# Chunked recurrences of a hybrid decoder step: the weights inside chunks computed in one run of 32-column matmuls per head

## Chip, cores and metric

One core of one Trainium2 chip. The metric is device microseconds (us) of one execution of the whole program, lower is better.

## What is computed

One inference step of a two-layer decoder for a prompt of 512 tokens and eight samples of 4 new tokens, 544 rows in all, width 2048. Layer A runs an attention (NSA) and a gated linear recurrence (GLA, 4 heads, key width 128, value width 256) side by side; layer C is HGRN2 (16 heads, key and value width 128). Both layers use this recurrence:

```python
def gated_recurrence(q, k, v, log_a, s0):
    """S_t = diag(exp(log_a_t)) S_{t-1} + k_t^T v_t, o_t = q_t S_t, per head"""
    ...
    def step(s, xs):
        qc, kc, vc, gc = xs
        b = jnp.cumsum(gc, axis=2)
        decay = jnp.exp(jnp.where(causal, b[:, :, :, None, :] - b[:, :, None, :, :], -jnp.inf))
        att = jnp.einsum('bhik,bhijk,bhjk->bhij', qc, decay, kc)
        o = jnp.einsum('bhij,bhjv->bhiv', att, vc) + jnp.einsum('bhik,bhkv->bhiv', qc * jnp.exp(b), s)
        b_last = b[:, :, -1:, :]
        s = jnp.exp(b_last)[:, :, 0, :, None] * s + jnp.einsum('bhjk,bhjv->bhkv', kc * jnp.exp(b_last - b), vc)
        return s, o
```

Around it stand the input projections `h @ w_in`, the output projections `o @ w_out`, root mean square norms and silu gates.

## The kernel before

**Layout.** Activations stand transposed, features in the 128 partitions and the 544 tokens along the free axis (`TP` = 512 prompt columns, `TS` = 32 sample columns). A big projection is a row of blocks of 128 output columns (`gemm_block`, L355). A block takes 16 K-tiles; a K-tile is six matmuls of 128x272 (weights split in a high and a low part, two halves of the tokens), so a block is 96 matmuls into a PSUM tile tagged `gm`. `stream` (L296) takes the weights in pieces of four K-tiles: it loads them in 512 KB transfers, splits each piece into `wh` (ScalarE) and `wl` (VectorE), and calls the split of piece n+2 ahead of the matmuls of piece n (`split_to(n + 3)`).

**Order of the work.** The program writes each engine's instructions in a fixed order, worked out while it is built. A planner clock `clk` follows TensorE: each matmul adds a cost (`mm`, L197), each VectorE or ScalarE operation has a modelled duration (`account`, L144). Every other job is a generator in a lane; `pump` is called behind each K-tile and steps the lanes whose wake time has come. A generator yields `self.at(tiles, banks=n)`: the modelled time at which these tiles are ready plus 200 ns, and n of the four small PSUM banks (tag `s`) are free. `together(gens, width)` (L688) interleaves up to `width` generators. TensorE therefore runs the long `gm` stream with short groups of small matmuls put in behind K-tiles.

**A head's recurrence** (`recurrence`, L713, called by `gla_task` and `hgrn_task` in lane H, one head after the other). The 512 prompt tokens are four chunks of 128. The lower triangle of weights inside a chunk is put together from levels, each a pair of factor tiles (differences of the cumulative log decay `b`, exponentials on ScalarE, products with `k` and `q` on VectorE), a group of small fp32 matmuls (each fp32 matmul is two records in the trace), and copies out of PSUM:

- `local` (L735): 4x4 blocks from factors `d` (a tile named `lv`) and `qh`; 16 matmuls of 32 stationary and 32 moving columns, and one for the samples into a second bank; masked copies into `attD` and `ats`.
- `level(4)` (L784): 16 matmuls of 32 by 16 columns; a masked copy into `attD`.
- `middle` (L828): 16 matmuls of 32 by 48 columns, moving tile `lq`; three masked copies into `attD`.
- `level(32)`: 8 matmuls of 32 by 32 columns; two copies into `attT`.
- `level(64)`: 4 matmuls of 64 by 64 columns; two copies into `attT`.

All of them use `tile_position=(0, 32 * g)`: the matmul occupies 32 (or 64) columns of the array from that position. Each level takes a bank of its own. `values` (L758) transposes the values and makes block-diagonal copies `vbd` for the samples; `passing` (L858) makes the factors that carry the state from chunk to chunk (`qe`, `ke`, `ket`, `kes`). The order is

```python
        gens = [local()] + [values(j) for j in range(nv)] + [level(4), middle(), level(32), level(64)] + [passing()]
        yield from self.together(gens, 3)
```

with four copies of `attD` onto the diagonal of `attT` behind it (L901), then the outputs (`prompt_out`, `sample_out`), the norm (`sq`, `sqh`, `sql`) and `y`. In layer C the first block of head h needs the flag of head h-2; the z block of head h-3 comes behind each head from the fourth on. Layer C ends with the z blocks of heads 13 to 15, and the output projection's last quarter needs the gated output of every head, split into `oh` and `ol`.

Of the kernel before, what the change touches and what calls it, by code (L numbers as in the profile page):

```python
# [20 lines left out]
P = 128  # L21
D = 2048
KT = D // P
TP = 512
NB = 8
NS = 4
TS = NB * NS
T = TP + TS
# [66 lines left out]
class Kern:  # L95
# [617 lines left out]
    def recurrence(self, q, k, la, vT, s0, out_p, out_s, gn, done):  # L713


        nc, ident = self.nc, self.ident
        nv = len(vT)
# [6 lines left out]
        attT, attD, ats = self.att  # L724
        yield self.at(la)
        b = self.r("b")
        nc.vector.tensor_tensor_scan(b, self.reset, la, 0.0, op0=ALU.mult, op1=ALU.add)

        d = self.r("lv")
# [3 lines left out]
        idb = [None]  # L733

        def local():  # L735
            yield self.at(d)
            qh = self.r("qh")
            nc.scalar.activation(qh, d, AF.Exp)
            nc.scalar.activation(d, d, AF.Exp, scale=-1.0)
            yield self.at(qh)  # L740
            self.tt(qh, qh, q, ALU.mult)
            yield self.at(d)
            self.tt(d, d, k, ALU.mult)
            yield self.at(d, qh, banks=2)
            ps, ps2 = self.bank(), self.bank()
            for c, g, rows, x in blocks32():
                self.mm(ps[rows, c * 32:(c + 1) * 32], d[:, x:x + 32], qh[:, x:x + 32], tile_position=(0, 32 * g))
            self.mm(ps2[:TS, :TS], d[:, TP:T], qh[:, TP:T])
            yield self.at(ps, attD)
            mk = self.lmask[1].unsqueeze(1).to_broadcast([P, 4, 32])  # L750
            nc.vector.copy_predicated(attD, mk, ps[:, :P].rearrange("p (c i) -> p c i", c=4))
            nc.vector.copy_predicated(ats, self.lmask[1][:TS], ps2[:TS, :TS])

        def blocks32():

            return [(c, g, slice(32 * g, 32 * g + 32), c * P + 32 * g) for c in range(4) for g in range(4)]

        def values(j):  # L758

            v3 = self.thrice(vT[j])  # L760
            yield self.at(vT[j], banks=1)
            ps = self.bank()
            for c in range(4):
                self.tr(ps[:, c * P:(c + 1) * P], vT[j][:, c * P:(c + 1) * P], ident)
            t = self.r("vt", [P, 4, P])
            self.cp(t, ps.rearrange("p (c d) -> p c d", c=4))
            vt.append(t)
            yield self.at(v3, banks=1)
            ps = self.bank(reads=3)
            self.tr(ps[:3 * TS, :P], v3, ident)  # L770
            t = self.sm("vs", [TS, P], bufs=2)
            nc.scalar.copy(t, ps[:TS, :P])
            vs.append(t)
            t = self.sm("v3", [3 * TS, P], bufs=2, dt=F32R)
            nc.scalar.copy(t, ps[:3 * TS, :P])
            yield self.at(t)
            nc.vector.tensor_tensor(t[2 * TS:], ps[2 * TS:3 * TS, :P], t[2 * TS:].bitcast(F32), op=ALU.subtract)
            for hf in range(2):
                vb = self.r("vbd", [P, 4, P], dt=F32R)
                self.tt(vb[:3 * TS], t.bitcast(F32).unsqueeze(1).to_broadcast([3 * TS, 4, P]),  # L780
                        self.bmask[:, hf * 4:hf * 4 + 4].unsqueeze(2).to_broadcast([3 * TS, 4, P]), ALU.mult)
                vbd.append(vb)

        def level(s):  # L784

            d = self.r("lv")
            v = lambda t: t[:, :TP].rearrange("p (n two s) -> p n two s", two=2, s=s)
            L, Rr = (lambda t: v(t)[:, :, 0, :]), (lambda t: v(t)[:, :, 1, :])
            n = 256 // s
            cb = v(b)[:, :, 0, s - 1:s].to_broadcast([P, n, s])  # L790
            nc.vector.tensor_tensor(Rr(d), Rr(b), cb, op=ALU.subtract)
            nc.vector.tensor_tensor(L(d), cb, L(b), op=ALU.subtract)
            yield self.at(d)
            nc.scalar.activation(d[:, :TP], d[:, :TP], AF.Exp)
            yield self.at(d)
            self.tt(L(d), L(d), L(k), ALU.mult)
            self.tt(Rr(d), Rr(d), Rr(q), ALU.mult)
            yield self.at(d, banks=1)
            ps = self.bank(reads=1 if s == 4 else 2)
            if s == 4:  # L800
                for c, g, rows, x in blocks32():
                    rr = d[:, x:x + 32].rearrange("p (n two s) -> p n two s", two=2, s=s)[:, :, 1, :]
                    self.mm(ps[rows, c * 16:(c + 1) * 16], d[:, x:x + 32], rr, tile_position=(0, 32 * g))
                yield self.at(ps, attD)
                nc.vector.copy_predicated(attD.rearrange("p c (n two s) -> p c n two s", two=2, s=s)[:, :, :, 1, :],
                                          self.lmask[4].unsqueeze(1).to_broadcast([P, 4, 4, 4]),
                                          ps[:, :64].rearrange("p (c n s) -> p c n s", c=4, s=s))
            elif s == 32:
                for c in range(4):
                    for g in (0, 2):  # L810
                        x = c * P + 32 * g
                        self.mm(ps[32 * g:32 * g + 32, c * 32:(c + 1) * 32], d[:, x:x + 32], d[:, x + 32:x + 64],
                                tile_position=(0, 32 * g))
                yield self.at(ps, attT)
                for r in (0, 64):
                    self.cp(attT[r:r + 32, :, r + 32:r + 64], ps[r:r + 32, :P].rearrange("p (c i) -> p c i", c=4))
            else:

                for c in range(4):
                    x, r = c * P, 64 * (c % 2)  # L820
                    self.mm(ps[r:r + 64, (c // 2) * 64:(c // 2) * 64 + 64], d[:, x:x + 64], d[:, x + 64:x + 128],
                            tile_position=(0, r))
                yield self.at(ps, attT)
                for r in range(2):
                    self.cp(attT[0:64].rearrange("p (a b) i -> p b a i", b=2)[:, r, :, 64:128],
                            ps[64 * r:64 * r + 64, :P].rearrange("p (c i) -> p c i", c=2))

        def middle():  # L828

            d, e = self.r("lv"), self.R.tile([P, 16, 48], F32, name=self.nm("lq"), tag="lq", bufs=1)  # L830
            b4 = b[:, :TP].rearrange("p (n m s) -> p n m s", m=4, s=8)
            bn = b[:, :TP].rearrange("p (n s) -> p n s", s=32)
            qn = q[:, :TP].rearrange("p (n s) -> p n s", s=32)
            nc.vector.tensor_tensor(d[:, :TP].rearrange("p (n m s) -> p n m s", m=4, s=8),
                                    b4[:, :, :, 7:8].to_broadcast([P, 16, 4, 8]), b4, op=ALU.subtract)
            quarters = [(0, 24), (24, 16), (40, 8)]
            for m, (x, w) in enumerate(quarters):
                nc.vector.tensor_tensor(e[:, :, x:x + w], bn[:, :, 32 - w:], bn[:, :, 8 * m + 7:8 * m + 8].to_broadcast([P, 16, w]),
                                        op=ALU.subtract)
            yield self.at(e)  # L840
            nc.scalar.activation(d[:, :TP], d[:, :TP], AF.Exp)
            nc.scalar.activation(e, e, AF.Exp)
            yield self.at(e)
            self.tt(d[:, :TP], d[:, :TP], k[:, :TP], ALU.mult)
            for x, w in quarters:
                self.tt(e[:, :, x:x + w], e[:, :, x:x + w], qn[:, :, 32 - w:], ALU.mult)
            yield self.at(d, e, banks=1)
            ps = self.bank(reads=3)
            for c, g, rows, x in blocks32():
                self.mm(ps[rows, c * 48:(c + 1) * 48], d[:, x:x + 32], e[:, 4 * c + g, :], tile_position=(0, 32 * g))  # L850
            yield self.at(ps, attD)
            for m, (x, w) in enumerate(quarters):
                nc.vector.copy_predicated(attD[:, :, 32 - w:], self.lmask[8][:, m:m + 1].unsqueeze(2).to_broadcast([P, 4, w]),
                                          ps[:, :192].rearrange("p (c i) -> p c i", c=4)[:, :, x:x + w])

        passed = {}

# [38 lines left out]
            yield self.at(kes)  # L896
            nc.vector.tensor_tensor(kes[TS:2 * TS], ps[TS:2 * TS, :P], kes[TS:2 * TS].bitcast(F32), op=ALU.subtract)

        gens = [local()] + [values(j) for j in range(nv)] + [level(4), middle(), level(32), level(64)] + [passing()]
        yield from self.together(gens, 3)  # L900
        yield self.at(attD, attT)  # L901
        for g in range(4):
            s = slice(32 * g, 32 * g + 32)
            self.cp(attT[s, :, s], attD[s])
        qe, dl, ket, kes = passed["qe"], passed["dl"], passed["ket"], passed["kes"]
        os_ = []

# [53 lines left out]
        gens = []  # L961
# [23 lines left out]
        for h in range(2):  # L985
            ps = self.bank()
# [1167 lines left out]
```

## Time and profile before

| | |
|---|---|
| runs | 2386.69, 2389.62, 2389.16 us; median 2389.16 |
| profiled execution | 2390.82 us, of it 2389.1 us span |
| TensorE granted clock, mean | 0.991 of full speed |
| TensorE matmul | 2341.7 us busy, 20560 records |
| VectorE / ScalarE | 1382.0 / 1022.8 us busy |
| DMA | mean 113 GB/s |

How to read it: a share over the span is a mean over stages. The timeline merges equal neighbours into one row (start, length, xcount); the length of such a row reaches to the end of its last record, and matmul ends are modelled and overlap the next start. Distances between starts are what can be added.

### The profile page before, as it was taken

How to read it: one execution, taken by the hardware profiler on the slowest of the kernel's cores; microseconds unless marked ns; L12 is line 12 of the kernel's file. 1: busy time of each engine (PE TensorE's matmuls, PEld its weight loads, DVE VectorE, ACT ScalarE, POOL GpSimd, SP SyncE). 2: the span in 40 equal slices, each digit the busy share in tenths (PEclk: the TensorE clock that was granted, in tenths of full speed). 3: DMA queues.
4: the chain of work that ended last, by engine and by line, in shares of the span. 5: the costliest groups of instructions: out<-in, count | busy, mean ns of one | idle time of the engine just before them, and what ended most of it. 6: DMA issues, size and time to landing. Idle time of an engine off the chain costs nothing.

```text
span 2389.1 us, 49910 instructions
## 1 busy us (share of the span) xinstructions
PE 2341.7 (98%) x20560; PEld 2247.9 (94%) x20560; DVE 1382.0 (58%) x2948; ACT 1022.8 (43%) x2152; POOL 25.7 (1%) x79
## 2 busy tenths in 40 slices
PE   7899999999999999999999999999999999999997
PEld 7799999999999988779999999999999999999997
DVE  5355567774664653354335667777777666665333
ACT  5244344443443443343333445544455444454333
POOL 3000000000000000000000000000000000000000
PEclk9899999999999999999999999999999999999999
DMA  7755434444213135454443233333333333333333
GB/s 247 241 161 158 124 99 109 106 111 119 54 50 89 43 108 163 147 164 134 134 124 98 85 98 101 92 98 90 91 98 94 95 91 91 98 90 113 99 113 111
DMA packets 433612, 270.68 MB, mean 113 GB/s; under 512 B 16285, under 2 KB 419640, under 8 KB 433256
## 3 DMA queue, kind: packets, MB, share of 16 engines
q1 hardware_dynamic: 432520, 257.05, 37.3%
q0 software_dynamic: 256, 8.32, 1.0%
q8 instruction: 162, 2.65, 0.5%
q10 hardware_dynamic: 608, 2.11, 0.2%
q14 instruction: 66, 0.54, 0.1%
HBM read 234.34 MB, written 41.42 MB: 115 GB/s over the span
## 4 chain that ended last, share of the span: by engine, by line
PE 93%; DVE 2%; DMA 1%; SPq 1%; ACT 1%; issue 1%; DVEq 0%; ACTq 0%
PE gm L211 77%; PE s L211 12%; PE s L215 4%; SPq L84 1%; DMA wr<-in_a_w_in_dram 1%; DVE ol L84 1%; DVE wl L84 1%; DMA xres<-res 0%; ACT sq L84 0%; ACT wh L84 0%; DMA wr<-in_a_w_out_dram 0%; ACT e L84 0%; DVE e L84 0%; ACT fr L84 0%; ACT qs L84 0%
## 5 line engine op out<-in xcount | busy, mean ns | idle before, releaser
L211 PE MATMUL gm<-xh,wh 128*128 128x272 f32 x3744 | 814.1, 299 | 1.9 <-ACT wh L84 1.9
L211 PE MATMUL gm<-xh,wl 128*128 128x272 f32 x3744 | 776.1, 289 | 2.7 <-DVE wl L84 2.7
L211 PE MATMUL gm<-xl,wh 128*128 128x272 f32 x3744 | 776.3, 289 | 0.0
L84 DVE TENSOR_TENSOR wl<-wr,wh 128x512 fp32r<-128x512 f32 x660 | 449.8, 686 | 492.4 <-ACT wh L84 491.1
L211 PEld LDWEIGHTS gm<-xh,wh 128*128 128x128 f32 x3744 | 587.1, 189 | 22.7 <-issue 11.6
L84 ACT CAST wh<-wr 128x512 fp32r<-128x512 f32 x660 | 402.4, 616 | 480.7 <-PE gm L211 459.8
L211 PEld LDWEIGHTS gm<-xh,wl 128*128 128x128 f32 x3744 | 588.2, 188 | 3.3 <-DVE wl L84 3.3
L211 PEld LDWEIGHTS gm<-xl,wh 128*128 128x128 f32 x3744 | 589.2, 188 | 0.0
L211 PE MATMUL gm<-oh,wh 128*128 128x272 f32 (+2 forms) x1024 | 219.4, 293 | 3.0 <-ACT oh L84 2.4
L211 PE MATMUL gm<-ol,wh 128*128 128x272 f32 (+2 forms) x1024 | 216.3, 290 | 2.4 <-DVE ol L84 2.4
L211 PE MATMUL gm<-oh,wl 128*128 128x272 f32 (+2 forms) x1024 | 215.7, 289 | 0.0
L211 PEld LDWEIGHTS gm<-oh,wh 128*128 128x128 f32 x1024 | 162.8, 190 | 4.0 <-ACT oh L84 2.9
L211 PEld LDWEIGHTS gm<-ol,wh 128*128 128x128 f32 x1024 | 163.2, 190 | 3.3 <-DVE ol L84 3.3
L211 PEld LDWEIGHTS gm<-oh,wl 128*128 128x128 f32 x1024 | 163.0, 190 | 0.0
L84 ACT ACTIVATE lv<-lv 128x512 f32<-128x512 f32 (+1 forms) x100 | 63.6, 637 | 110.2 <-DVE lv L84 109.5
L211 PE MATMUL gm<-ch,wh 128*128 128x258 f32 (+1 forms) x256 | 76.7, 300 | 1.3 <-ACT ch L84 1.3
L211 PE MATMUL gm<-cl,wh 128*128 128x258 f32 (+1 forms) x256 | 76.8, 300 | 0.8 <-DVE cl L84 0.8
L211 PE MATMUL gm<-ch,wl 128*128 128x258 f32 (+1 forms) x256 | 76.6, 299 | 0.0
L84 DVE TENSOR_TENSOR lv<-b 128x256 f32<-128x256 f32 (+2 forms) x160 | 72.5, 483 | 0.7
L84 ACT ACTIVATE e<-e 128x544 f32<-128x544 f32 x96 | 63.1, 658 | 20.1 <-DVE e L84 18.1
L84 ACT COPY o<-s 128x32 f32<-128x32 f32 (+1 forms) x47 | 18.0, 382 | 108.8 <-PE s L211 108.8
L84 DVE TENSOR_TENSOR rt<-gm,rt 128x544 f32<-128x544 f32 (+2 forms) x33 | 23.4, 708 | 62.2 <-PE gm L211 62.2
(372 smaller groups left out, 2566.8 us busy)
## 6 DMA issues: line engine op xcount, KB each, us to landing
wr<-in_c_w_in_dram SPq DMA_DIRECT2D x128, 512.0 KB
wr<-in_a_w_in_dram SPq DMA_DIRECT2D x104, 512.0 KB
pg<-in_cache_kv_dram SPq DMA_DIRECT2D x128, 128.0 KB
wr<-in_a_cmp_w_dram SPq DMA_DIRECT2D x32, 512.0 KB
wr<-in_a_w_out_dram SPq DMA_DIRECT2D x32, 512.0 KB
wr<-in_c_w_out_dram SPq DMA_DIRECT2D x32, 512.0 KB
out_dram<-s SPq DMA_DIRECT2D x48, 256.0 KB
pw<-in_cache_win_dram SPq DMA_DIRECT2D x32, 256.0 KB
```

Of the source, the lines that this page charges most:

```text
L84: return f(*args, **kw)
L211: return self.nc.tensor.matmul(out, lhsT, rhs, start=start, stop=stop, **kw)
L215: return self.nc.tensor.transpose(out, in_, ident, **kw)
```

## The change

The levels and `local` stop behind their factors and leave the factor tiles in a dictionary `fac`. A new generator `products` waits for all of them and two banks, issues every small matmul in one go into banks A and B, and then makes the copies, the four diagonal ones among them. `level(64)`'s four matmuls of 64 stationary columns become eight of 32. The matmul for the samples gets a tile position. The generators run in two groups: the factors first, then `products`, `values` and `passing`.

```diff
@@ local @@
             self.tt(d, d, k, ALU.mult)
-            yield self.at(d, qh, banks=2)
-            ps, ps2 = self.bank(), self.bank()
...
+            fac[1] = (d, qh)
+            d = None
@@ level @@
             self.tt(Rr(d), Rr(d), Rr(q), ALU.mult)
-            yield self.at(d, banks=1)
-            ps = self.bank(reads=1 if s == 4 else 2)
...
+            fac[s] = (d,)
@@ middle @@
-            yield self.at(d, e, banks=1)
-            ps = self.bank(reads=3)
...
+            fac[8] = (d, e)
+
+        def products():
+
+            yield self.at(*[t for ts in fac.values() for t in ts], banks=2)
+            A, B = self.bank(reads=7), self.bank(reads=3)
+            d, qh = fac[1]
+            for c, g, rows, x in blocks32():
+                self.mm(A[rows, c * 32:(c + 1) * 32], d[:, x:x + 32], qh[:, x:x + 32], tile_position=(0, 32 * g))
+            self.mm(B[:TS, P:P + TS], d[:, TP:T], qh[:, TP:T], tile_position=(0, 0))
+            d, = fac[4]
...
+                self.mm(A[rows, 128 + c * 16:128 + (c + 1) * 16], d[:, x:x + 32], rr, tile_position=(0, 32 * g))
+            d, e = fac[8]
+            for c, g, rows, x in blocks32():
+                self.mm(A[rows, 192 + c * 48:192 + (c + 1) * 48], d[:, x:x + 32], e[:, 4 * c + g, :],
+                        tile_position=(0, 32 * g))
+            d, = fac[32]
...
+            d, = fac[64]
+            for c in range(4):
+                for hf in range(2):
+                    x, r = c * P, 64 * (c % 2) + 32 * hf
+                    self.mm(B[r:r + 32, (c // 2) * 64:(c // 2) * 64 + 64], d[:, x + 32 * hf:x + 32 * hf + 32],
+                            d[:, x + 64:x + 128], tile_position=(0, r))
+            fac.clear()
+            del d, e, qh
+            yield self.at(A, B, attD, attT)
...
+            yield self.at(attD, attT)
+            for g in range(4):
+                s = slice(32 * g, 32 * g + 32)
+                self.cp(attT[s, :, s], attD[s])
@@ end of the factors @@
-        gens = [local()] + [values(j) for j in range(nv)] + [level(4), middle(), level(32), level(64)] + [passing()]
-        yield from self.together(gens, 3)
-        yield self.at(attD, attT)
-        for g in range(4):
-            s = slice(32 * g, 32 * g + 32)
-            self.cp(attT[s, :, s], attD[s])
+        fac = {}
+        yield from self.together([local(), level(4), middle(), level(32), level(64)], 3)
+        yield from self.together([products()] + [values(j) for j in range(nv)] + [passing()], 3)
```

## Rows read from the trace of the kernel before

**Rows 1.** Page: busy us, share of the span, instructions; chain that ended last

```profile
PE 2341.7 (98%) x20560; PEld 2247.9 (94%) x20560; DVE 1382.0 (58%) x2948; ACT 1022.8 (43%) x2152; POOL 25.7 (1%) x79
PE 93%; DVE 2%; DMA 1%; SPq 1%; ACT 1%; issue 1%; DVEq 0%; ACTq 0%
```

**Rows 2.** Groups by line and form, TensorE: xcount, busy us, mean ns

```profile
L211 PE MATMUL s<-lq,lv 128*32 128x48 f32 x640 | 11.0, 209 | 0.0
```

**Rows 3.** Timeline of TensorE, first head of layer C: start us, length us

```profile
1301.37 0.50 PE L211 MATMUL s<-qh,lv 128*32 128x32 f32 x34
1301.80 0.52 PE L211 MATMUL gm<-xh,wh 128*128 128x272 f32 x2
...
1305.78 0.45 PE L211 MATMUL s<-lv 128*32 128x16 f32 x32
1306.16 0.52 PE L211 MATMUL gm<-xh,wh 128*128 128x272 f32 x2
...
1310.52 0.41 PE L211 MATMUL gm<-xh,wl 128*128 128x272 f32 x2
1310.87 0.55 PE L211 MATMUL s<-lq,lv 128*32 128x48 f32 x32
1311.34 0.52 PE L211 MATMUL gm<-xh,wh 128*128 128x272 f32 x2
1311.70 0.41 PE L211 MATMUL gm<-xl,wh 128*128 128x272 f32 x2
1311.95 0.41 PE L211 MATMUL gm<-xh,wl 128*128 128x272 f32 x2
1312.29 0.45 PE L211 MATMUL s<-lv 128*32 128x32 f32 x16
1312.67 0.52 PE L211 MATMUL gm<-xh,wh 128*128 128x272 f32 x2
...
1315.12 0.45 PE L211 MATMUL s<-lv 128*64 128x64 f32 x8
1315.50 0.52 PE L211 MATMUL gm<-xh,wh 128*128 128x272 f32 x2
```

**Rows 4.** The same timeline around four full-width transposes

```profile
1341.63 0.42 PE L211 MATMUL gm<-xh,wl 128*128 128x272 f32 x2
1341.88 0.60 PE L215 MATMUL s<-ident,ci 128*128 128x128 f32 x4
...
1342.58 0.41 PE L211 MATMUL gm<-xl,wh 128*128 128x272 f32 x2
```

**Rows 5.** The same timeline: two other groups of 32-column matmuls

```profile
868.16 0.86 PE L211 MATMUL s<-kv,qd 128*32 128x32 f32 x64
...
1321.64 0.64 PE L211 MATMUL s<-s,qz 128*32 128x128 f32 x16
```

**Rows 6.** Busy by stretch (PE, PEld, DVE, ACT); timelines of DVE and TensorE

```profile
1298.00:1313.00 15.00, 15.00 (x216) 14.23 (x215) 14.81 (x38) 7.50 (x17) 0.00 (x0) 1.00 0.26 75
...
1311.48 0.76 DVE L84 COPY_PREDICATED attD<-lm,s 128x96 f32<-128x96 uint32 x3
...
1312.48 0.42 DVE L84 TENSOR_TENSOR lv<-lv,cq 128x256 f32<-128x256 f32 x1
...
337.35 0.41 DVE L84 TENSOR_TENSOR lv<-lv,gq 128x256 f32<-128x256 f32 x1
...
338.45 0.45 PE L211 MATMUL s<-lv 128*32 128x16 f32 x32
```

**Rows 7.** Waits of TensorE: us in total, times, longest

```profile
PE gm L211 <- ACT oh L84: 2.4, 1, 2.4
...
PE s L215 <- DVE thr L84: 1.4, 2, 0.9
```

**Rows 8.** Timeline of DVE: end of head 13's recurrence, evacuation of head 15's q

```profile
2043.98 0.78 DVE L84 SCALAR_TENSOR_TENSOR y<-o,cvec,sq 128x544 f32<-128x544 f32 x1
...
2084.82 0.72 DVE L84 TENSOR_TENSOR cq<-gm,rstd 128x544 f32<-128x544 f32 x1
```

More of the change, by code (lines that the diff above doesn't have):

```diff
@@ L735, in local @@
         def local():
+            nonlocal d
             yield self.at(d)
@@ L743, in local @@
             self.tt(d, d, k, ALU.mult)
-            yield self.at(d, qh, banks=2)
-            ps, ps2 = self.bank(), self.bank()
[L746 to L752, printed above, removed]
+            fac[1] = (d, qh)
+            d = None
         def blocks32():
@@ L797, in level @@
             self.tt(Rr(d), Rr(d), Rr(q), ALU.mult)
-            yield self.at(d, banks=1)
-            ps = self.bank(reads=1 if s == 4 else 2)
[L800 to L826, printed above, removed]
+            fac[s] = (d,)
         def middle():
@@ L846, in middle @@
                 self.tt(e[:, :, x:x + w], e[:, :, x:x + w], qn[:, :, 32 - w:], ALU.mult)
-            yield self.at(d, e, banks=1)
-            ps = self.bank(reads=3)
-            for c, g, rows, x in blocks32():
-                self.mm(ps[rows, c * 48:(c + 1) * 48], d[:, x:x + 32], e[:, 4 * c + g, :], tile_position=(0, 32 * g))
-            yield self.at(ps, attD)
-            for m, (x, w) in enumerate(quarters):
-                nc.vector.copy_predicated(attD[:, :, 32 - w:], self.lmask[8][:, m:m + 1].unsqueeze(2).to_broadcast([P, 4, w]),
-                                          ps[:, :192].rearrange("p (c i) -> p c i", c=4)[:, :, x:x + w])
+            fac[8] = (d, e)
@@ new lines, in products @@
+        def products():
+            yield self.at(*[t for ts in fac.values() for t in ts], banks=2)
+            A, B = self.bank(reads=7), self.bank(reads=3)
+            d, qh = fac[1]
+            for c, g, rows, x in blocks32():
+                self.mm(A[rows, c * 32:(c + 1) * 32], d[:, x:x + 32], qh[:, x:x + 32], tile_position=(0, 32 * g))
+            self.mm(B[:TS, P:P + TS], d[:, TP:T], qh[:, TP:T], tile_position=(0, 0))
+            d, = fac[4]
+            for c, g, rows, x in blocks32():
+                rr = d[:, x:x + 32].rearrange("p (n two s) -> p n two s", two=2, s=4)[:, :, 1, :]
+                self.mm(A[rows, 128 + c * 16:128 + (c + 1) * 16], d[:, x:x + 32], rr, tile_position=(0, 32 * g))
[5 more added lines that the diff above has]
+            for c in range(4):
+                for g in (0, 2):
+                    x = c * P + 32 * g
+                    self.mm(A[32 * g:32 * g + 32, 384 + c * 32:384 + (c + 1) * 32], d[:, x:x + 32], d[:, x + 32:x + 64],
+                            tile_position=(0, 32 * g))
+            d, = fac[64]
+            for c in range(4):
+                for hf in range(2):
[5 more added lines that the diff above has]
+            yield self.at(A, B, attD, attT)
+            v = lambda t, w: t.rearrange("p (c i) -> p c i", c=4)
+            nc.vector.copy_predicated(attD, self.lmask[1].unsqueeze(1).to_broadcast([P, 4, 32]), v(A[:, :P], 32))
+            nc.vector.copy_predicated(attD.rearrange("p c (n two s) -> p c n two s", two=2, s=4)[:, :, :, 1, :],
+                                      self.lmask[4].unsqueeze(1).to_broadcast([P, 4, 4, 4]),
+                                      A[:, 128:192].rearrange("p (c n s) -> p c n s", c=4, s=4))
+            for m, (x, w) in enumerate([(0, 24), (24, 16), (40, 8)]):
+                nc.vector.copy_predicated(attD[:, :, 32 - w:], self.lmask[8][:, m:m + 1].unsqueeze(2).to_broadcast([P, 4, w]),
+                                          v(A[:, 192:384], 48)[:, :, x:x + w])
+            nc.vector.copy_predicated(ats, self.lmask[1][:TS], B[:TS, P:P + TS])
+            for r in (0, 64):
+                self.cp(attT[r:r + 32, :, r + 32:r + 64], v(A[r:r + 32, 384:], 32))
+            for r in range(2):
+                self.cp(attT[0:64].rearrange("p (a b) i -> p b a i", b=2)[:, r, :, 64:128],
+                        B[64 * r:64 * r + 64, :P].rearrange("p (c i) -> p c i", c=2))
+            yield self.at(attD, attT)
+            for g in range(4):
+                s = slice(32 * g, 32 * g + 32)
+                self.cp(attT[s, :, s], attD[s])
```

## The prediction

> **What bounds the kernel now.** I read the page first: TensorE is busy over 98% of the span, and the chain that ended last is 93% TensorE [rows 1]. A microsecond less on TensorE is then a microsecond less of time, unless TensorE meets a wait in its place. The next view is the timeline of TensorE around a head's small matmuls, where distances between starts show what each group costs the long `gm` stream. Without interruption two `gm` records take 0.25 us (1311.70 to 1311.95) [rows 3]. In the first head of layer C each of the five groups stands alone between `gm` records, and all 20 heads (4 of layer A, 16 of layer C) show the same pattern; the moving tile `lq` for one has 640 records, 32 a head [rows 2].
>
> Take the group of `middle`. From the pair before it (1310.52) to the second pair after it (1311.70) pass 1.18 us, and two pairs would take 0.50, so the group costs 0.68 us [rows 3]. It splits like this:
> - Entry: the group starts 0.35 us after the pair before it, not 0.25; 0.34 before the group at 1312.29.
> - Stream: its row is 0.55 us long and one record lasts 0.21 [rows 2, 3], so its last record starts 0.34 us after its first, a stride of 11 ns for 31 steps.
> - Exit: 0.47 us after the first start comes the next `gm` pair, 0.13 behind the last small start, and that pair takes 0.36 instead of 0.25.
>
> So about 0.10 + 0.11 us are lost at the edges and 0.12 (0.13 less one stride) at the drain: some 0.32 us of the 0.68 don't depend on what the group holds. The others confirm it: from their start to the next `gm` pair pass 0.43, 0.38, 0.38 and 0.38 us [rows 3], with the same edges (0.20) added 0.63, 0.58, 0.58 and 0.58. The group at 1315.12 has 8 records and costs as much as the one with 32 at 1305.78. One head pays 0.68 + 0.63 + 3 x 0.58 = 3.05 us, 20 heads 61 us. Four full-width transposes in the same stream cost no such edge: 1341.63 to 1342.58 is 0.95 us, less two pairs 0.45, 0.11 for each [rows 4]. The fixed part belongs to the narrow form, not to the interruption.
>
> **The change part by part.**
>
> *One run in place of five groups.* Four entries and exits of 0.32 us go: 1.28 us a head, 25.6 us in all, on TensorE and so on the path. The streams stay, 3.05 - 5 x 0.32 = 1.45 us, in one go of 34 + 32 + 32 + 16 + 16 = 130 records. Whether the four joins inside the run cost something the trace does not show. Below, nothing; above, a whole fixed part each (0.32). I take nothing: the run keeps 32 columns of the array throughout, and the stride inside the 34 and inside the 32 is near 10 ns whichever widths are used.
>
> *Level 64: 8 records of 64 stationary columns become 16 of 32.* Its stream was 0.58 - 0.32 = 0.26 us. The new one lies between 16 records with 48 moving columns (half of 0.34: 0.17) and 16 with 128 (0.64 less one record of 0.28: 0.36) [rows 3, 5]. By columns 64 is near the lower, about 0.21. I take no difference; the ends are -0.09 and +0.10 a head, -1.8 and +2.0 us in all.
>
> *A rule against the strides.* The rows give strides of 9 to 11 ns for groups up to 34 records [rows 3], and 64 records in a row of 0.86 us, less one of 0.2, a stride of 10.5 ns [rows 5]. The Trainium skill (TensorE: Matmul & The Clock Gate, section "Wait — 56ns, not 53.3ns?") states that start to start never drops below about 25 ns however small the matmul is; by an estimate from it the run of 130 would last 3.3 us and a head would cost 3.6 us, more than now, about 10 us slower in all. The trace contradicts this for up to 64 records; longer runs no row shows (last rival).
>
> *Factors first.* VectorE and ScalarE do the same factor work and the same ten copies a head. What moves: the values' operations go behind the factors, the small matmuls behind the last factor. VectorE is the engine to watch, 14.81 of 15 us busy in this stretch [rows 6]. The run waits for the latest of six tiles. `level(64)` now has 2.2 us in hand (its last product ends at 1312.90, its group starts at 1315.12) [rows 3, 6]; the first heads of layer A have less, 0.7 us from the end of `lv<-lv,gq` at 337.76 to the group at 338.45, and other products stand between [rows 6]. With the values' work out of VectorE's queue the last factor comes sooner, so I price this wait at nothing in most heads; if the cover is gone, TensorE stops for the difference in every head.
>
> *The copies in one bunch.* The masked copies (0.76 us for the three of `middle` [rows 6], the other three smaller) come together, behind the whole run. Behind them on VectorE wait the `wl` splits, which TensorE needs; the split of piece n+2 is issued ahead of piece n, and a piece is 24 matmuls, 3.0 us by the 0.25 us pair, so 6 us cover a bunch of about 1.5. Banks A and B stay taken until the copies are done; two of four remain for the transposes of `values` and `passing`, which come later on the planner's clock, not on TensorE's. No DMA is added; the loads of `S0` stay ahead of everything, and the stores move with the outputs on SP's queue, which nothing waits on.
>
> *The recurrence's length.* The flag that releases head h+2 has room: head 13 ends at 2044.8, and head 15's q is evacuated at 2084.8; its 96 matmuls take 12 us, so its block starts near 2071 with some 26 us to spare [rows 8]. A few microseconds more of latency cost nothing there.
>
> *What is late next.* TensorE waits 2.4 us for `oh` once, at the end of layer C, for the last gated outputs on VectorE and ScalarE [rows 7]. The last head's 1.28 us only lengthens that wait. Early in layer C, where no z block is there yet, it waits twice for `thr`, 1.4 us [rows 7]; there too a faster TensorE waits longer, some 1.1 us in all. Together 2.4 us given back.
>
> **Sum**: 25.6 - 0 - 2.4 = 23.2 us. The profiled execution took 2390.8 us, 1.7 over the median of the runs shown (2389.2). Against the median: 2366 us, 1.0% faster.
>
> **The rivals.**
> 1. *Given back as waits.* VectorE is full in this stretch, and the run starts only with the last factor, so TensorE may stop in front of it in every head. For: the 14.81 of 15 us. Against: 2.2 us in hand. At half of the saving, 0.64 us a head, 12.8 us remain: 2376 us.
> 2. *The joins cost what the edges cost*, because the width changes and not the interruption. For: no row shows two widths side by side. Against: entry and exit are the same for 8 records and for 34. Then nothing changes: 2389 us.
> 3. *Slower: the run is too long for what stands ready in TensorE's queue.* Small matmuls go by fast where their instructions already wait behind the `gm` stream; a run of 130 may use these up and then go at the pace of supply. For: the longest narrow row has 64 [rows 5]. Against: that row shows no lower pace, 10.5 ns. It decides for the 66 records beyond the 64th, from the pace at which they eat the saving: 1.28 / 66 + 0.011 = 30 ns. The pace lies between 11 ns and the transposes' 110 [rows 4]; at 35 ns, in the middle by ratio, a head loses 1.6 and gains 1.28 us, 6 us in all: 2395 us; at 110 it would be near 2495. By the 25 ns of the Trainium skill (TensorE: Matmul & The Clock Gate, same section), taken as that pace, a head would lose 66 x 0.014 = 0.9 us and a third of the gain would be left.
>
> **How the numbers follow.** Forecast 0.70, rival 1 0.14, rival 2 0.08, rival 3 0.08. The predicted time is the forecast's, 2366 us. Low end: nothing given back, level 64 at its better end, and a run as far under its median as the lowest shown (2.5 us): 2389.2 - 27.4 - 2.5 = 2359. High end: half given back and level 64 at its worse end leave 10.8 us, 2378, and a little spread, 2380; that holds the forecast and most of rival 1. A measurement of this kernel can tell about 0.2%, 4.8 us. Forecast and nearly all of rival 1 are faster by more: 0.83. Rival 2 and the rest are within it: 0.09. Rival 3: 0.08 slower.
>
> **What would show it.** Right: one narrow group of 130 records a head, about 1.45 us from first to last start, then one `gm` pair of 0.36 us, and the head 1.3 us shorter. Rival 1: a gap with a VectorE or ScalarE releaser in front of the run, or `gm` waits for `wl`. Rival 2: gaps of 0.1 to 0.3 us where the width changes. Rival 3: the stride grows behind about the 64th record. The forecast is wrong if TensorE's waits grow by over 10 us, or if the run lasts over 2.7 us.

## The result, and the profile after

| | before | after |
|---|---|---|
| median of 4 runs, us | 2388.73 (2386.69 to 2389.62) | 2357.66 (2355.87 to 2358.77) |
| profiled execution, its span, us | 2390.82, 2389.1 | 2358.77, 2357.1 |
| ratio after / before, 95% interval | | 0.987 (0.9858 to 0.9883) |

The change makes the kernel 31.1 us faster. The direction and the mechanism were forecast, the size was not: 2366 us was predicted, and the measured time lies below the low end of the range, 2359.

The page of the changed kernel, as in [rows 1], with the line of the instruction queue from its part on DMA queues (packets, MB, share of 16 engines), which the last experiments need:

```profile
PE 2312.2 (98%) x20720; PEld 2234.0 (95%) x20720; DVE 1397.2 (59%) x2999; ACT 1008.0 (43%) x2101; POOL 25.9 (1%) x79
q8 instruction: 163, 2.67, 0.5%
PE 94%; DVE 1%; DMA 1%; SPq 1%; ACT 1%; issue 0%; DVEq 0%; ACTq 0%
```

TensorE has 160 records more (level 64 in narrower pieces) and 29.5 us less of busy time, and it is still the path. VectorE has 51 instructions and 15 us more, ScalarE 51 fewer: the planner handed other evacuations to VectorE. Nothing waits on that.

The timeline of TensorE around the first head of layer C, which answers to [rows 3]:

```profile
1304.58 0.41 PE L211 MATMUL gm<-xh,wl 128*128 128x272 f32 x2
1304.92 0.47 PE L211 MATMUL s<-qh,lv 128*32 128x32 f32 x33
...
1305.88 0.64 PE L211 MATMUL s<-lv 128*32 128x32 f32 x31
1306.45 0.32 PE L215 MATMUL s<-ident,thr 128*96 128x128 f32 x1
1306.53 0.50 PE L211 MATMUL gm<-xh,wh 128*128 128x272 f32 x2
1306.86 0.41 PE L211 MATMUL gm<-xl,wh 128*128 128x272 f32 x2
```

One narrow group a head is left. It enters as each of the five did before, 0.34 us behind the pair ahead of it. The last row of the run is 0.64 us long and one of its records lasts 0.22, so the last start is at 1306.30, 1.38 us behind the first: 130 records at a mean stride of 10.7 ns; the 32 of levels 32 and 64 stand at the end (named together here, x31). All 20 heads show 1.385 to 1.387 us. Behind the run comes a transpose of the values (`thr`, 96 of 128 columns), not a `gm` pair.

The chain of waits gives the length of a head, since with TensorE always busy the same stretch of `gm` matmuls comes back once a head. Start, length and number of matmuls; first the kernel before (a stretch of 156 that ends at the next narrow group), three heads apart:

```profile
1870.37 19.63 PE gm L211 x156
...
2041.49 19.60 PE gm L211 x156
```

and after (a stretch of 240), four heads apart:

```profile
1848.52 30.17 PE gm L211 x240
...
2071.32 30.20 PE gm L211 x240
```

A head takes 171.12 / 3 = 57.04 us before and 222.80 / 4 = 55.70 after: 1.34 us less, 26.8 us if all 20 heads gain as much as these. The rest of the 32.0 us between the two spans is in the waits and in TensorE's clock. Before, TensorE's waits have these rows beside those of [rows 7]:

```profile
PE s L215 <- DMA pg<-in_cache_kv_dram: 8.6, 3, 6.8
...
PE gm L211 <- DVE wl L84: 2.7, 2, 1.5
```

and after:

```profile
PE s L215 <- DMA pg<-in_cache_kv_dram: 9.8, 3, 7.8
...
PE gm L211 <- DVE ol L84: 2.7, 4, 1.9
...
PE gm L211 <- ACT oh L84: 1.6, 1, 1.6
...
PE gm L211 <- DVE wl L84: 1.2, 1, 1.2
```

There is no row for `thr` any more (1.4 in [rows 7]), `wl` fell by 1.5 us, `oh` by 0.8, and `ol` rose by 0.3 (2.4 before). Of the other rows the wait for the DMA of `pg` rose by 1.2, `snt` by 0.2 (1.8 to 2.0), and `res` fell by 0.9 (2.4 to 1.5). All rows together went from 36.8 to 33.9 us: 2.9 us less of waiting.

Behind the wait for `oh` the clock differs as well. Before, first the timeline, then the same place by stretch (as in [rows 6]: the number after the engines is the granted clock):

```profile
2181.38 0.82 PE L211 MATMUL gm<-oh,wh 128*128 128x272 f32 x2 [2.44 <-ACT oh L84]
...
2187.72 0.41 PE L211 MATMUL gm<-ol,wh 128*128 128x272 f32 x2
...
2180.84:2187.67 6.83, 6.29 (x26) 6.04 (x27) 3.15 (x5) 2.28 (x4) 0.00 (x0) 0.50 0.34 105
```

and after:

```profile
2152.01 0.52 PE L211 MATMUL gm<-oh,wh 128*128 128x272 f32 x2 [1.64 <-ACT oh L84]
...
2155.89 0.41 PE L211 MATMUL gm<-ol,wh 128*128 128x272 f32 x2
...
2150.00:2160.00 10.00, 8.12 (x63) 7.66 (x63) 4.96 (x8) 3.93 (x8) 0.00 (x0) 1.00 0.45 133
```

In the kernel before, TensorE had stood still for 2.44 us when it went on at 2181.38; from 2180.84 to 2187.67 the granted clock is 0.50, the lower of its two levels, and 13 steps from pair to pair take 6.34 us. In the changed kernel the stop is 1.64 us, the clock stays at 1.00, and 13 steps take 3.88 us, 0.24 of it a wait for `ol` that is counted above. That is another 2.7 us. The lower level's other stretches, all ahead of 1080 us but for the one at the very end, add up to 23.9 us in both kernels. So 26.8 + 2.9 + 2.7 = 32.4 us stand against the 32.0 measured.

Where the `wl` wait went is seen on VectorE, in the first head of layer A. Before, start and length:

```profile
328.38 1.29 DVE L84 TENSOR_TENSOR vbd<-v,bm 96x512 fp32r<-96x512 f32 x2
...
330.00 1.29 DVE L84 TENSOR_TENSOR vbd<-v,bm 96x512 fp32r<-96x512 f32 x2
...
334.25 1.28 DVE L84 TENSOR_TENSOR wl<-wr,wh 128x512 fp32r<-128x512 f32 x2
```

After, the same microseconds:

```profile
330.40 0.68 DVE L84 TENSOR_TENSOR wl<-wr,wh 128x512 fp32r<-128x512 f32 x1
...
333.95 0.68 DVE L84 TENSOR_TENSOR wl<-wr,wh 128x512 fp32r<-128x512 f32 x1
```

The four `vbd` products of the values (2.6 us) stood in VectorE's queue ahead of the factors and of the `wl` splits; a split was ready only near 334.9, and TensorE stood still for 1.5 us. With the values' work behind the factors the splits come at 330.4 and 334.0, and TensorE does not wait there.

### The profile page after: what moved, and what is told of

It is laid out like the page before. It is cut to its first block, busy times and chain, and to the rows that moved or that the text cites. A ratio compares the mean times of both kernels' runs of the same rounds, so it can differ in the third digit from the quotient of the medians.

```text
span 2357.1 us, 50145 instructions
## 1 busy us (share of the span) xinstructions
PE 2312.2 (98%) x20720; PEld 2234.0 (95%) x20720; DVE 1397.2 (59%) x2999; ACT 1008.0 (43%) x2101; POOL 25.9 (1%) x79
## 3 DMA queue, kind: packets, MB, share of 16 engines
q8 instruction: 163, 2.67, 0.5%
## 4 chain that ended last, share of the span: by engine, by line
PE 94%; DVE 1%; DMA 1%; SPq 1%; ACT 1%; issue 0%; DVEq 0%; ACTq 0%
PE gm L211 79%; PE s L211 12%; PE s L215 4%; SPq L84 1%; DVE ol L84 1%; DMA xres<-res 0%; DMA xt<-in_x_prompt_dram 0%; DMA wr<-in_a_w_in_dram 0%; ACT oh L84 0%; DMA pg<-in_cache_kv_dram 0%; ACT e L84 0%; DVE wl L84 0%; DVE e L84 0%; ACT wh L84 0%; DMA out_dram<-snt 0%
## 5 line engine op out<-in xcount | busy, mean ns | idle before, releaser
L211 PE MATMUL gm<-xh,wh 128*128 128x272 f32 x3744 | 803.7, 296 | 1.9 <-ACT wh L84 1.9
```

Of the source, the lines that this page charges most:

```text
L211: return self.nc.tensor.matmul(out, lhsT, rhs, start=start, stop=stop, **kw)
```

## The experiments

Two theories on the 31 us went into the first runs. **Theory 1**: nearly all of it is the edges, so that the number of narrow groups sets the time, whatever their order. The rival: it is the new order (factors first, values later) that takes work out of TensorE's way. All times below are medians, with a 95% interval on the ratio to the kernel before.

**Five groups in the new order.** Everything of the change stays, but a pause for the planner stands ahead of each of the four later groups, so that `gm` pairs come between them again:

```diff
@@ products(), ahead of the loops over fac[4], fac[8], fac[32] and fac[64]
+            yield self.later(100.0)
```

> The changed kernel with its order kept (all factors first, values behind them), but the one run of 130 records taken apart into the five groups again, with full-width work between them. Theory 1 (the saving is the four entries and exits of the narrow form, 0.32 us each): 20 heads x 4 x 0.32 = 26 us come back, 2384 us; what is left of the gain, about 5 us, is the waits that went. Theory 2 (the saving comes from the new order of factors, values and copies, the grouping matters little): within 5 us of the changed kernel, 2358 to 2363 us.

Measured: 2385.35 us, ratio 0.9986 (0.9977 to 0.9996), 10 runs. With five groups the saving is gone: 27.7 of the 31.1 us hang on the single run, 3.0 on the order (before was 2388.37 beside these runs). The chain, two heads apart:

```profile
1923.53 30.91 PE gm L211 x246
...
2037.31 30.91 PE gm L211 x246
```

56.89 us a head. So the order alone gives 0.15 us a head, and one run in place of five groups 1.19, against the 1.28 predicted for it. The timeline shows one place where some of the 0.15 may come from:

```profile
1617.92 0.50 PE L211 MATMUL s<-qh,lv 128*32 128x32 f32 x34
1618.35 0.31 PE L215 MATMUL s<-ident,thr 128*96 128x128 f32 x1
1618.60 0.45 PE L211 MATMUL s<-lv 128*32 128x16 f32 x32
```

In the new order a transpose is due just then and stands between narrow groups in place of `gm` pairs; it shares an edge with them. That this is all of the 0.15 is not shown. Not all of the 27.7 us is edges: 20 x 1.19 = 24 us, and the waits of this kernel are longer than those of the changed one, `oh` by 2.1 us (here too the granted clock is 0.50 for 6.8 us behind it) and a new one for `ke`:

```profile
PE gm L211 <- ACT oh L84: 3.7, 2, 2.6
...
PE s L215 <- DVE ke L84: 2.2, 3, 0.9
```

**Two groups.** The same pause once, ahead of level 32: a group of 98 records and one of 32.

```diff
@@ products()
+            yield self.later(100.0)
             d, = fac[32]
```

> The changed kernel with its run cut once, in front of the groups of level 32 and level 64. Theory 1: one more entry and exit a head, 20 x 0.32 = 6.4 us more than the changed kernel, about 2364 us, a quarter of what cutting it in five costs. Rival (a run loses only where it is interrupted by a wait or by a new bank, so one cut is free): 2358 us.

Measured: 2366.91 us, ratio 0.9906 (0.9889 to 0.9922), 4 runs. The timeline of one head:

```profile
1664.09 0.41 PE L211 MATMUL gm<-xh,wl 128*128 128x272 f32 x2
1664.43 0.47 PE L211 MATMUL s<-qh,lv 128*32 128x32 f32 x33
...
1665.51 0.31 PE L215 MATMUL s<-ident,thr 128*96 128x128 f32 x1
1665.75 0.67 PE L211 MATMUL s<-lv 128*32 128x32 f32 x32
...
1666.71 0.41 PE L211 MATMUL gm<-xl,wh 128*128 128x272 f32 x2
```

From the pair ahead of the run to the second pair behind it pass 2.62 us, with one transpose inside. The changed kernel does the same work in 2.28 (1304.58 to 1306.86 above). A cut costs 0.34 us, close to the fixed part of 0.32 that the prediction read from one head of the kernel before. Twenty cuts make 6.8 of the 9.3 us that this kernel is slower than the changed one; its `oh` wait is 2.1 us longer as well, and the granted clock is 0.50 for 3.4 us behind it.

**The values early again, in layer C.** The single run stays; the values' generator goes back among the factors (layer C alone: with two value tiles a head, layer A's recurrence doesn't have the buffers for it).

```diff
-        yield from self.together([local(), level(4), middle(), level(32), level(64)], 3)
-        yield from self.together([products()] + [values(j) for j in range(nv)] + [passing()], 3)
+        yield from self.together([local()] + ([values(0)] if nv == 1 else []) + [level(4), middle(), level(32), level(64)], 3)
+        yield from self.together([products()] + ([values(j) for j in range(nv)] if nv > 1 else []) + [passing()], 3)
```

> The changed kernel with the generator of the values back among the factors, in layer C only; the one run stays. Theory A (the waits for thr in the first heads of layer C went because the values' transposes moved behind the factors): 1.4 to 1.7 us of waits for thr come back, 2359 to 2360 us, the run of 130 unchanged. Theory B (they went because VectorE's queue got shorter through the copies being made in one bunch): no wait for thr, 2358 us. Theory 2 of the first run (order is what saves): 10 us or more come back.

Measured: 2360.11 us, ratio 0.988 (0.9863 to 0.9896), 2.5 us slower than the changed kernel measured first, 4.1 slower than the control below. From the waits of TensorE:

```profile
PE s L215 <- DVE thr L84: 1.8, 2, 1.3
```

The wait for `thr` is back, and twice, as in [rows 7]. So the vanished `thr` wait is the work of the order, not of the run. It is longer than before (1.8 against 1.4), the way the prediction said of a faster TensorE; but the change moved the work that it waits for.

**Level 64 in its old form.** Four matmuls of 64 stationary columns at the end of the run in place of eight of 32 (in records, 8 in place of 16):

```diff
-                for hf in range(2):
-                    x, r = c * P, 64 * (c % 2) + 32 * hf
-                    self.mm(B[r:r + 32, (c // 2) * 64:(c // 2) * 64 + 64], d[:, x + 32 * hf:x + 32 * hf + 32],
-                            d[:, x + 64:x + 128], tile_position=(0, r))
+                x, r = c * P, 64 * (c % 2)
+                self.mm(B[r:r + 64, (c // 2) * 64:(c // 2) * 64 + 64], d[:, x:x + 64], d[:, x + 64:x + 128],
+                        tile_position=(0, r))
```

> The changed kernel with level 64 as four matmuls of 64 stationary columns again, at the end of the same run. Theory 1a (the edge belongs to any change of the form, 32 to 64 columns included): one more edge of up to 0.2 to 0.3 us a head, 4 to 6 us more, 2362 to 2364 us. Theory 1b (the edge belongs to going between full width and narrow): the difference of the two streams alone, 0.23 against about 0.20 us, under 1 us in all, 2358 us.

Measured: 2360.89 us, ratio 0.9884 (0.9868 to 0.9901), 3.2 us slower than the changed kernel, with fewer instructions. The chain, four heads apart:

```profile
1846.77 30.17 PE gm L211 x240
...
2070.08 30.20 PE gm L211 x240
```

55.83 us a head, 0.13 more than the 55.70 of the changed kernel, 2.6 us in all. The run's first to last start grows from 1.386 to 1.540 us. Level 64 itself takes the same from its first start to its last, 0.230 us for 8 records here and 0.228 for 16 in the changed kernel: a gap of 101 ns inside the 8 stands in the kernel before as well (100 ns), where they are a group of their own. What is new, by the starts of the single records in all 20 heads, is the gap of 126 ns ahead of the first 64-column record, where the changed kernel has 5. A change of column width inside a run costs some 0.13 us, less than a cut (0.34) and not nothing. That the change writes level 64 in 32 columns spares its run this one join. The measured 3.2 us are not the 2.6 alone: the `oh` wait is 2.1 us longer here (3.7), while the stretches at the lower clock ahead of the end add up to 17.1 us in place of 23.9.

**A control and two attempts to go further.** The changed kernel itself ran again beside the next two.

> The changed kernel itself, once more, so that the two versions beside it have it on the same chip: 2356 to 2359 us by every theory.

Measured: 2356.04 us, ratio 0.9861 (0.9844 to 0.9877), so two measurements of one kernel lie 1.6 us apart.

The first attempt asks whether the edge belongs to the 32 rows of a stationary tile as to its 32 columns. In the changed kernel the two `ats` matmuls (32 rows) follow the group of `qz`:

```profile
1670.83 0.64 PE L211 MATMUL s<-s,qz 128*32 128x128 f32 x16
1671.41 0.40 PE L211 MATMUL s<-ats,vs 32*128 32x32 f32 x2
1671.74 0.52 PE L211 MATMUL gm<-xh,wh 128*128 128x272 f32 x2
```

The edit pads `ats` and `vs` to 96 rows (zeros in `ats`) and issues the matmul ahead of the `qz` group:

```diff
-            t = self.sm("vs", [TS, P], bufs=2)
-            nc.scalar.copy(t, ps[:TS, :P])
+            t = self.sm("vs", [3 * TS, P], bufs=2)
+            nc.scalar.copy(t, ps[:3 * TS, :P])
...
+            self.mm(pso[:, :TS], vs[j], ats)
             for s in range(2):
...
-            self.mm(pso[:, :TS], vs[j], ats)
```

> The changed kernel with the samples' product of weights and values (32 contraction rows, between the 32-column group of qz and the gm stream) made with 96 rows, 64 of them zero in the weights, and put ahead of that group. Theory 1 (every change of the array's form costs its edge, by rows as by columns): from the last full-width record before the group to the second gm record behind it 1.34 us now, 1.16 us then, 0.18 us for each of 24 groups, 4.4 us less than the changed kernel, about 2353 us. Rival (the 0.2 us around that product are its own latency, not an edge): nothing, 2358 us.

Measured: **2352.06 us**, ratio 0.9847 (0.983 to 0.9863), 4.0 us less than the control. It beats both kernels.

```profile
1665.75 0.31 PE L211 MATMUL s<-ats,vs 96*128 96x32 f32 x2
1665.98 0.64 PE L211 MATMUL s<-s,qz 128*32 128x128 f32 x16
1666.56 0.52 PE L211 MATMUL gm<-xh,wh 128*128 128x272 f32 x2
```

From the start of `qz` to the first `gm` pair pass 0.91 us in the changed kernel and 0.58 here, where the two `ats` records have gone ahead of it in 0.23: 0.1 us less between these rows, the rest at the edge in front of them: from the last full-width record ahead of the two to the first `gm` record behind them pass 1.11 us there and 0.92 here, within 0.02 us in all 24 groups. By the chain (1841.98 and 2063.96 us, four heads apart) a head takes 55.50 us, 0.20 less; with two value tiles a head in layer A that makes 24 x 0.2 = 4.8 us, of which 4.0 were measured. The edit changes two things, the rows and the place; which of the two brings the gain was not tried apart. In its new place the tile of 96 rows shows no edge: it starts 0.11 to 0.13 us behind the full-width record ahead of it, as those start behind each other.

The second attempt builds on the first and moves the `qz` group itself into the run, which becomes 146 records long in layer C and 162 in layer A:

```diff
@@ products(), behind fac[64]
+            for j in range(nv):
+                for s in range(2):
+                    for jj in range(4):
+                        self.mm(B[32 * jj:32 * jj + 32, 160 + j * P:160 + (j + 1) * P], self.qz[:, jj, s, :], S0[j][s][:, jj, :],
+                                start=(s == 0), stop=(s == 1), tile_position=(0, 32 * jj))
```

(and a generator `queries()` among the factors, which computes `qz` in time).

> The same, and the group of qz itself (16 records of 32 columns for each half of the values) moved into the run of 130, its result into bank B; the factors qe and qz are made with the other factors. Theory 1: with no group of its own left, 0.46 us less for each of 24 groups than in the changed kernel, 11 us in all, about 2347 us. Rival (the run now waits for more on a full VectorE, and the copies get longer): half of it is eaten by waits in front of the run, 2352 us or more. Supply theory (a run of 146 to 162 records goes slower behind some length): the stride grows, 2358 us or more.

Measured: 2356.66 us, ratio 0.9865 (0.9849 to 0.9882): 4.6 us slower than the first attempt, where a gain had been expected. The timeline of one head, and a row of the waits of TensorE that the other kernels' lists hardly have (0.4 us at most):

```profile
1395.32 0.42 PE L211 MATMUL s<-s,qz 128*32 128x128 f32 x6
1397.09 0.49 PE L211 MATMUL s<-s,qz 128*32 128x128 f32 x9 [1.35 <-issue]
```

```profile
PE s L211 <- issue: 4.4, 6, 1.4
```

In 6 of the 16 heads of layer C the run stops inside, for 0.47 to 1.62 us, and always at its 128th to 144th record. TensorE waits for nothing that the profile shows ("issue"). In these six heads a packet of the instruction queue begins within 0.6 us of the run's start, in the other ten none within 1.9. A packet is 2.67 MB / 163 = 16.4 KB, and 2 x 20720 records of TensorE over 163 packets make 254 records, 127 records of matmuls with their weight loads. That looks like rival 3 of the prediction, behind the 128th record and not behind the 64th; none of the four runs of 162 in layer A stops, so length alone does not decide. The six stops add up to 6.0 us. They are not the whole of the loss: a head is shorter than in the first attempt where the run does not stop (55.1 against 55.5 us), but the waits grew too, `oh` from 1.6 to 3.1 us and a new one of 1.4 for `ke`, as the rival on record said.

**The run twice.** All matmuls of a run issued twice into the same columns, 260 records a head, the rest unchanged.

```diff
@@ products()
+            for _ in range(2):
                 d, qh = fac[1]
...
```

> Issues all matmuls of the run of a head twice (the second pass writes the same columns with the same products again), so that a run has 260 TensorE records where the changed kernel has 130; nothing else differs. Supply theory: a run longer than some 130 records meets the end of what was fetched into TensorE's queue, as the runs of 146 and 162 records did in some heads; 260 records are more than one packet of the instruction queue (about 254 records), so every head should show a stop of 0.5 to 1.6 us inside its run, the run should take over 3.2 us, and the total should be above 2395 us. Rival, no limit of supply: the run takes 2 x 1.39 = 2.8 us in every head and the total is 2357.7 + 20 x 1.39 = 2385.5 us, within 3 us.

Measured: 2475.36 us (one run; 2388.87 for the kernel before beside it). The timeline of one head, the row of the waits, and the page's line of the instruction queue:

```profile
1476.74 0.47 PE L211 MATMUL s<-qh,lv 128*32 128x32 f32 x33
...
1479.11 0.50 PE L211 MATMUL s<-lv 128*32 128x32 f32 x17
1483.47 0.65 PE L211 MATMUL s<-lv 128*32 128x64 f32 x14 [3.86 <-issue]
```

```profile
PE s L211 <- issue: 57.7, 20, 4.1
```

```profile
q8 instruction: 183, 3.00, 0.5%
```

The rival's 2385 us is out. Every one of the 20 runs stops once, at its 149th to 250th record, for 1.65 to 4.27 us. Up to there the stride is as before: 246 records go in 2.65 us in this head (1476.74 to 1479.39). 20 packets more for 5200 records more (2600 of matmuls and 2600 of weight loads) make 260 a packet; the expectation set the 254 of a packet against the 260 matmul records of a run and left out the weight loads, so that a run here is two packets and not one. In each head TensorE goes on 2.3 to 2.9 us behind the start of the latest packet, and no two packets start less than 3.4 us apart. A packet holds some 127 matmul records, and a narrow run uses it up in 1.4 us. So what limits such a run is by all signs the supply of instructions: the stops keep time with the packets, and every run that is two packets long has one, though no run changed the supply alone. The price on record (above 2395 us) was far too low. The stops are longer than in the runs of 146, and behind them the clock falls. For the head above, by stretch:

```profile
1482.73:1489.56 6.83, 6.09 (x39) 5.92 (x39) 3.93 (x10) 2.87 (x10) 0.00 (x0) 0.50 0.01 2
```

The granted clock is 0.50 for 3.4 or 6.8 us in 16 of the 20 heads, beginning between 1.4 us ahead of the end of the stop and 1.6 us behind it, 68 us together; a `gm` pair then takes 0.45 us in place of 0.25, so by an estimate from these numbers some 30 us are lost. With 27.8 us for the second pass and 57.7 for the stops that makes about 116 us, and the two spans lie 116.6 us apart (2473.7 and 2357.1). What sets the moment at which the next packet starts, from 0.6 us ahead of the stop to 1.9 us into it, stays open.

The Trainium skill (Runtime: NRT & Kernel Launch, section "Instruction fetch mechanics") states that instructions come in blocks of 16 KiB, 256 of them, and that the cost of crossing from one block into the next is mostly hidden. The traces agree with the size of a block (254 to 260 records). "Mostly hidden" holds for the 20 runs of the changed kernel; 6 runs of 146 records and all 20 of 260 stop.

## Why the prediction was wrong

By the steps of the prediction:

- **One run in place of five groups**: right. The joins cost nothing, the stream took 1.39 us (1.45 forecast), a cut costs 0.34 (0.32). 26.8 us came of it where 25.6 were forecast; of these, 0.15 us a head come with the new order, perhaps from the transposes that now share an edge, which the prediction didn't see.
- **Level 64**: taken at no difference, and right: from first to last start 0.230 us before, 0.228 after. What the 32 columns spare is a join of two widths inside the run, 0.13 us a head, which the prediction didn't price.
- **A rule against the strides**: the trace was the one to believe. The run lasts 1.39 us, a mean of 10.7 ns a record over all 130. The Trainium skill (TensorE: Matmul & The Clock Gate, section "Wait — 56ns, not 53.3ns?") states 25 ns as the least from start to start; by an estimate from it the run would last 3.3 us, and the trace does not agree.
- **Factors first, the copies in one bunch, the recurrence's length**: priced at nothing, and no wait came. None of the 20 runs has a stop in front of it, `wl` waits fell. What was overlooked is that the first of them could give something.
- **What is late next** is the step that failed. It said that 2.4 us are given back: the `oh` wait longer by 1.3 us, the two `thr` waits by 1.1. In fact the waits of TensorE shrank by 2.9 us: `thr` -1.4, `wl` -1.5, `oh` -0.8, `ol` +0.3, the others together +0.5. With the shorter stop for `oh` went 6.8 us at the lower clock, 2.7 us more, which stood behind that stop before and which the prediction's price for it left out. The step kept the work that those waits wait for where it was and made TensorE earlier. But the change moves that work too: the values' transposes and products go behind the factors, TensorE reaches `thr` later than its producer, and VectorE reaches the `wl` splits sooner. For `thr` this is shown (with the values early the wait came back, 1.8 us), for `wl` the two timelines of VectorE show it in one place. Why the `oh` wait at the end of layer C became shorter and not longer, and with it why no stretch at the lower clock follows, is not settled: over all kernels run, its longest stop lies between 1.6 and 2.7 us, in no order that their edits explain.

The sum: 23.2 us were forecast and 32.0 came between the two profiled executions. Of the 8.8 us between them, 1.2 are the heads, 2.4 + 2.9 = 5.3 the waits and 2.7 the clock; that is 0.4 more than was measured.

**The rivals.** Given back as waits: none stands in front of a run. The joins cost what the edges cost: 1.39 us for the whole run speaks against it, and the cut kernels show that it is the interruption that costs; a join of two column widths would have cost 0.13, and the run has none. The slower one names a mechanism that longer runs bear out, at another place: the prediction let the supply of instructions decide behind the 64th record, and the runs of 146 and 260 stop behind the 128th. The changed kernel stands just inside: two of its heads (at 1394.7 and 1443.1 us) have a packet that begins within 0.5 us of the run, and their 130 records go through, while one head of the kernel with the values early (at 1445.8) stopped at its 121st record for 0.67 us, and one of the kernel with two groups (at 1721.8) at the end of its second group for 0.51. In the control's 20 runs no gap is longer than 0.07 us.

**The range** had its low end at "nothing given back". It allowed for no gain from waits or from the clock behind them, though the change moves the work that the listed `thr` wait names.

## What to carry to other kernels

Narrow-tile matmuls inside a full-width stream pay a fixed price for each interruption beside the 10.7 ns a record: here a third of a microsecond each time, whatever the group holds, so bring them together in one run, and give every tile the same column width. Look at the packets of the instruction queue before such a run grows: with some 127 matmul records to a packet, runs of 130 went through here, but for one, 6 of 16 of 146 records stopped, and all of 260. Price a stop of TensorE with the clock behind it: read the granted clock of the stretch that follows. When a change moves work in a queue, go through the list of waits by name and ask of each whether its producer moved, before taking for granted that a faster engine waits longer.

## What the runs showed that was not expected

- The stop of long narrow runs: up to 4.27 us, with a steady 10.7 ns until then. More records in a run (the `qz` group, 16) cost more in stops and waits than the edge they save.
- The clock behind a stop: at the lower level a `gm` pair takes 0.45 us, and that makes some 30 us of the cost of the doubled runs and 2.7 us of the gain of the change.
- The two records on a stationary tile of 32 rows behind the `qz` group cost some 0.2 us more each time than the same product on 96 rows ahead of it. The padding and the new place together gave the best time, 2352.06 us.
- A change from 32 to 64 columns inside a run costs 0.13 us, where a cut costs 0.34.
